# Rotary embedding: GpSimd's two products per tile become one, and the last position is stored as 126 and 2 rows

## The chip, the cores and the metric

The kernel runs on one core of a Trainium2 chip. The metric is the device time of one execution in microseconds, lower is better. Most of it is the span, from the first to the last instruction in the profile.

## The reference

Each row of 64 numbers is cut into two halves of 32 and rotated by an angle that depends on its position alone:

```python
# x: (8, 2048, 8, 64) f32; cos, sin: (2048, 32) f32
x1, x2 = x[..., :32], x[..., 32:]
out1 = x1 * cos - x2 * sin
out2 = x1 * sin + x2 * cos
return np.concatenate([out1, out2], axis=-1)
```

Input and output are 33.55 MB each and every element of x is read once, so the work is two products and one sum per element beside the transfers.

## The kernel before

**Layout.** Each of the 8 batches is one tile of 128 partitions. Partition q holds 16 neighbouring positions (R = 16), a position holds 8 heads of 64 numbers (HD = 512 elements, 2 KB), so a partition's row of a batch is 8192 elements, 32 KB, contiguous in HBM. The unit of computing is UNIT = 4 positions, 2048 elements per partition. The first batch starts with two half units and the last one ends with two half units.

**Tables.** cos_sb, sin_sb and nsin (minus sine) lie in SBUF, 16 x 32 elements per partition. cos_ps and sin_ps are copies in PSUM. ScalarE makes nsin (L90), sin_ps (L91) and neye (L92, minus the identity matrix); VectorE makes cos_ps (L93).

**One tile.** The function rotate computes t1 = x * cos for all elements on VectorE (L129), and t2 = the other half times the signed sine on GpSimd in two products (L122): the second halves of t2 from the first halves of x and sin_sb, then the first halves of t2 from the second halves of x and nsin. Each product writes 32 of every 64 elements and repeats the table over the 8 heads. Then out = t1 + t2, in the place of x. There are three kinds of tile:

- A, the most: VectorE adds (L136).
- B, the first tile of batches 2, 4 and 5: TensorE adds by two products with the identity matrix (L143, L144), ScalarE copies the sum from PSUM (L145).
- C, the first tile of batches 1 and 3: VectorE makes t2 too (L148), TensorE adds (L160, L161), ScalarE copies (L165). GpSimd has no part in it.

**Order of the work.** Every instruction keeps its place in the program's order on its engine. All loads of x are issued by SP (L67), the load of cos after the first of them (L69); sin is loaded by ScalarE's queue (L76). Five batches fit in SBUF (NBUF = 5); the load of batch b + 5 waits until the store of batch b has landed. Stores (L74) are issued by ScalarE's queue, one for a whole batch of 4 MB, except that batch 0 is stored in three parts. The last batch is stored by SP, in parts of 8, 4 and 4 positions, each when the pieces that it covers are done. At the end (L219) SP waits for all stores to have landed.

Of the kernel before, what the change touches and what calls it, by code (L numbers as in the profile page):

```python
# [9 lines left out]
@with_exitstack  # L10
def kernel(
    ctx: ExitStack,
    tc: tile.TileContext,
    x: bass.AP,
    cos: bass.AP,
    sin: bass.AP,
    out: bass.AP,
):
    nc = tc.nc
    keep = tc.keep_in_program_order  # L20
    f32 = mybir.dt.float32
    PSUM = bass.MemoryType.PSUM

    B, S, H, D = x.shape
    Dh = D // 2
    P = 128
    HD = H * D
    R = S // P
    ROW = R * HD
    UNIT = 4 * HD  # L30
    NBUF = 5
    C = 512
    last = B - 1

    xv = x.rearrange("b (q r) h d -> b q (r h d)", q=P)
    ov = out.rearrange("b (q r) h d -> b q (r h d)", q=P)
    cos_src = cos.rearrange("(q r) d -> q r d", q=P)
    sin_src = sin.rearrange("(q r) d -> q r d", q=P)

    const_pool = ctx.enter_context(tc.tile_pool(name="const", bufs=1))  # L40
    tab_pool = ctx.enter_context(tc.tile_pool(name="tab", bufs=1, space=PSUM))
    t1_pool = ctx.enter_context(tc.tile_pool(name="t1p", bufs=1, space=PSUM))
    o_pool = ctx.enter_context(tc.tile_pool(name="op", bufs=1, space=PSUM))
    t1s_pool = ctx.enter_context(tc.tile_pool(name="t1s", bufs=2))
    xpool = ctx.enter_context(tc.tile_pool(name="xpool", bufs=NBUF))
    t2_pool = ctx.enter_context(tc.tile_pool(name="t2p", bufs=3))

    cos_sb = const_pool.tile([P, R, Dh], f32, tag="cb")
    sin_sb = const_pool.tile([P, R, Dh], f32, tag="sb")
    nsin = const_pool.tile([P, R, Dh], f32, tag="ns")  # L50
    eye = const_pool.tile([P, P], f32, tag="eye")
    neye = const_pool.tile([P, P], f32, tag="neye")
    cos_ps = tab_pool.tile([P, R, Dh], f32, tag="cp")
    sin_ps = tab_pool.tile([P, R, Dh], f32, tag="sp")

    xts = {}

    def spans(sizes):
        lo = 0
        for n in sizes:  # L60
            yield lo, n
            lo += n

    def load(b):
        xt = xpool.tile([P, ROW], f32, tag="xt", name=f"xt{b}")
        for lo, n in spans([UNIT, UNIT, 2 * UNIT] if b == 0 else [ROW]):
            keep(nc.sync.dma_start(out=xt[:, lo : lo + n], in_=xv[b, :, lo : lo + n]))  # L67
            if b == 0 and lo == 0:
                keep(nc.sync.dma_start(out=cos_sb, in_=cos_src))  # L69
        xts[b] = xt  # L70

    def store(b, lo, n):
        queue = nc.sync if b == last else nc.scalar
        keep(queue.dma_start(out=ov[b, :, lo : lo + n], in_=xts[b][:, lo : lo + n]))  # L74

    keep(nc.scalar.dma_start(out=sin_sb, in_=sin_src))  # L76
    for b in range(NBUF):
        load(b)

    keep(nc.gpsimd.memset(eye, 0.0))  # L80
    nc.gpsimd.affine_select(
        out=eye,
        in_=eye,
        compare_op=mybir.AluOpType.not_equal,
        fill=1.0,
        base=0,
        pattern=[[-1, P]],
        channel_multiplier=1,
    )
    keep(nc.scalar.mul(nsin, sin_sb, -1.0))  # L90
    keep(nc.scalar.copy(sin_ps, sin_sb))  # L91
    keep(nc.scalar.mul(neye, eye, -1.0))  # L92
    keep(nc.vector.tensor_copy(cos_ps, cos_sb))  # L93

    def rep(a, n):
        return dataclasses.replace(a, ap=[a.ap[0][:], a.ap[1][:], [0, n], a.ap[-1][:]])

    kinds = {}
    for b, kind in ((1, "C"), (2, "B"), (3, "C"), (4, "B"), (5, "B")):
        kinds[(b, 0)] = kind  # L100

    def rotate(b, lo, n):
        kind = kinds.get((b, lo), "A")
        xt = xts[b][:, lo : lo + n]
        r0 = lo // HD
        nr = n // HD
        xk = xt.rearrange("p (r k d) -> p r k d", r=nr, d=Dh)
        xu = xt.rearrange("p (g u d) -> p g u d", u=2, d=Dh)
        if kind == "A":
            t1 = t1_pool.tile([P, n], f32, tag="t1")  # L110
        else:
            t1 = t1s_pool.tile([P, n], f32, tag="t1s")
        if kind == "C":
            t2 = t1s_pool.tile([P, n], f32, tag="t1s")
        else:
            t2 = t2_pool.tile([P, n], f32, tag="t2")
        t1u = t1.rearrange("p (g u d) -> p g u d", u=2, d=Dh)
        t2u = t2.rearrange("p (g u d) -> p g u d", u=2, d=Dh)
        if kind != "C":
            for u, tab in ((1, sin_sb), (0, nsin)):  # L120
                keep(
                    nc.gpsimd.tensor_mul(  # L122
                        out=t2u[:, :, u, :].rearrange("p (r h) d -> p r h d", h=H),
                        in0=xu[:, :, 1 - u, :].rearrange("p (r h) d -> p r h d", h=H),
                        in1=rep(tab[:, r0 : r0 + nr, :], H),
                    )
                )
        keep(
            nc.vector.tensor_mul(  # L129
                out=t1.rearrange("p (r k d) -> p r k d", r=nr, d=Dh),  # L130
                in0=xk,
                in1=rep(cos_ps[:, r0 : r0 + nr, :], 2 * H),
            )
        )
        if kind == "A":
            keep(nc.vector.tensor_add(out=xt, in0=t1, in1=t2))  # L136
        elif kind == "B":
            for j in range(n // (2 * C)):
                o = o_pool.tile([P, 2 * C], f32, tag="o")
                for k in range(2):  # L140
                    cs = slice((2 * j + k) * C, (2 * j + k + 1) * C)
                    oc = o[:, k * C : (k + 1) * C]
                    nc.tensor.matmul(oc, eye, t1[:, cs], start=True, stop=False)  # L143
                    nc.tensor.matmul(oc, eye, t2[:, cs], start=False, stop=True)  # L144
                keep(nc.scalar.copy(xt[:, 2 * j * C : 2 * (j + 1) * C], o))  # L145
        else:
            keep(
                nc.vector.tensor_mul(  # L148
                    out=t2.rearrange("p (r k d) -> p r k d", r=nr, d=Dh),
                    in0=xk,  # L150
                    in1=rep(sin_ps[:, r0 : r0 + nr, :], 2 * H),
                )
            )
            G = C // Dh
            for u in range(2):
                o = o_pool.tile([P, n // 2], f32, tag="o")
                for j in range(n // 2 // C):
                    oc = o[:, j * C : (j + 1) * C]
                    gs = slice(j * G, (j + 1) * G)
                    nc.tensor.matmul(oc, eye, t1u[:, gs, u, :], start=True, stop=False)  # L160
                    nc.tensor.matmul(  # L161
                        oc, eye if u else neye, t2u[:, gs, 1 - u, :], start=False, stop=True
                    )
                keep(
                    nc.scalar.copy(  # L165
                        xu[:, :, u, :], o.rearrange("p (g d) -> p g d", d=Dh)
                    )
                )

    def pieces(b):  # L170
        if b == 0:
            return [2 * HD, 2 * HD, UNIT, UNIT, UNIT]
        if b == last:
            return [UNIT, UNIT, UNIT, 2 * HD, 2 * HD]
        return [UNIT] * 4

    def shares(b):
        if b == 0:
            return [UNIT, UNIT, 2 * UNIT]
        if b == last:  # L180
            return [2 * UNIT, UNIT, UNIT]
        return [ROW]

    for b in range(B):
        done = 0
        outs = list(spans(shares(b)))
        for lo, n in spans(pieces(b)):
            rotate(b, lo, n)
            done = lo + n
            while outs and sum(outs[0]) <= done:  # L190
                store(b, *outs.pop(0))
        if b + NBUF <= last:
            load(b + NBUF)
# [30 lines left out]
```

## Time and profile before

| | |
|---|---|
| time, median of 3 runs | 163.39 us (163.34 to 163.5) |
| time of the profiled execution | 163.35 us |
| its span | 161.5 us |
| instructions in the span | 460 |
| HBM read and written | 34.08 MB and 33.55 MB, 419 GB/s over the span |
| VectorE, product with cos on 2048 elements (L129) | x30, 68.5 us, 2291 ns each |
| VectorE, sum on 2048 elements (L136) | x25, 57.3 us, 2292 ns each |
| GpSimd, product with sin_sb on 1024 elements (L122) | x28, 66.2 us, 2365 ns each, 3.2 us idle before |
| GpSimd, product with nsin on 1024 elements (L122) | x28, 66.3 us, 2368 ns each |
| VectorE's waits for GpSimd before L136 | 1.2 us, 2 times |
| last sum of VectorE begins | 150.98 us, 1.23 us long |
| last parts of the last batch, from issue to landing | 13.5 us for 2 MB; 9.9 us (median of two) for 1 MB |

Times inside the profile count from the start of the span. The time of a run is longer than the span by what lies around it, 163.35 - 161.5 = 1.85 us in the profiled execution. The 16 DMA engines of the core share every transfer: a store of 128 rows shows 16 completions. GpSimd's instructions overlap a little in the records, so what counts for its speed is the distance from one start to the next.

### The profile page before, as it was taken

The numbers are of one execution on the slowest core, as the hardware profiler recorded it, in microseconds if no ns is written. First come the engines' busy times: TensorE is split into PE (matmuls) and PEld (weight loads), VectorE is DVE, ScalarE is ACT, GpSimd is POOL, SyncE is SP. The second block draws the span as 40 slices with busy tenths as digits, with TensorE's granted clock in tenths as the row PEclk, the third lists the DMA queues.
The fourth block names the chain that finished last, engine by engine and source line by source line (L and its number), as shares of the span: only waits on it lengthen the run. The fifth ranks groups of instructions, "written<-read, shape, count | busy, mean of one in ns | idle before, by whom it ended". The sixth has DMA issues, their size and how long they took to land.

```text
span 161.5 us, 460 instructions
## 1 busy us (share of the span) xinstructions
PE 49.2 (30%) x80; PEld 18.5 (11%) x80; DVE 140.1 (87%) x66; ACT 12.8 (8%) x14; POOL 138.9 (86%) x70
## 2 busy tenths in 40 slices
PE   0000000597309770978039723973000000000000
PEld 0000000142004220323023302320000000000000
DVE  0297999999999999999999999999999999999600
ACT  3300000002200220021100220022000000000000
POOL 1399997999999999999994999999999999996000
PEclk9999999999975998589956995599655555555555
DMA  5999998998999999999999999999999999999994
GB/s 153 423 458 418 430 487 381 430 487 381 487 398 446 389 462 389 462 446 389 487 422 389 487 416 389 487 422 398 473 422 406 471 422 406 471 422 406 426 404 209
DMA packets 3458, 67.65 MB, mean 419 GB/s; under 512 B 384, under 2 KB 384, under 8 KB 640
## 3 DMA queue, kind: packets, MB, share of 16 engines
q1 hardware_dynamic: 2016, 38.01, 55.3%
q10 hardware_dynamic: 1440, 29.62, 42.8%
q14 instruction: 2, 0.02, 0.0%
HBM read 34.08 MB, written 33.55 MB: 419 GB/s over the span
## 4 chain that ended last, share of the span: by engine, by line
DVE 75%; POOL 9%; issue 6%; DMA 4%; DVEq 0%
DVE t L129 40%; DVE xt L136 33%; POOL t L122 9%; DMA sin_sb<-in_sin_dram 4%; DVE t L148 3%; DVEq L136 0%
## 5 line engine op out<-in xcount | busy, mean ns | idle before, releaser
L122 POOL TENSOR_TENSOR t<-xt,sin_sb 128x1024 f32<-128x1024 f32 (+1 forms) x32 | 71.2, 2226 | 8.5 <-DMA sin_sb<-in_sin_dram 5.3
L129 DVE TENSOR_TENSOR t<-xt,cos_ps 128x2048 f32<-128x2048 f32 (+1 forms) x34 | 73.4, 2166 | 0.8
L122 POOL TENSOR_TENSOR t<-xt,nsin 128x1024 f32<-128x1024 f32 (+1 forms) x32 | 71.3, 2228 | 0.0
L136 DVE TENSOR_TENSOR xt<-t,t 128x2048 f32<-128x2048 f32 (+1 forms) x29 | 62.2, 2145 | 4.2 <-POOL t L122 1.2
L143 PE MATMUL o<-t,eye 128*128 128x512 f32 x24 | 16.9, 797 | 23.1 <-DVE t L129 19.7
L160 PE MATMUL o<-t,eye 128*128 128x512 f32 x16 | 12.0, 842 | 37.9 <-DVE t L129 35.7
L144 PE MATMUL o<-t,eye 128*128 128x512 f32 x24 | 14.9, 709 | 0.0
L145 ACT COPY xt<-o 128x1024 f32<-128x1024 f32 x6 | 6.1, 1012 | 45.7 <-PE o L144 45.7
L143 PEld LDWEIGHTS o<-t,eye 128*128 128x128 f32 x24 | 5.5, 256 | 32.5 <-issue 26.6
L160 PEld LDWEIGHTS o<-t,eye 128*128 128x128 f32 x16 | 3.7, 256 | 43.4 <-issue 39.5
L165 ACT COPY xt<-o 128x1024 f32<-128x1024 f32 x4 | 4.0, 1012 | 47.8 <-PE o L161 47.8
L93 DVE COPY cos_ps<-cos_sb 128x512 f32<-128x512 f32 x1 | 0.7, 695 | 7.1 <-DMA cos_sb<-in_cos_dram 7.1
L144 PEld LDWEIGHTS o<-t,eye 128*128 128x128 f32 x24 | 5.6, 235 | 8.1 <-issue 8.1
L161 PE MATMUL o<-t,neye 128*128 128x512 f32 x8 | 6.2, 872 | 0.2
L148 DVE TENSOR_TENSOR t<-xt,sin_ps 128x2048 f32<-128x2048 f32 x2 | 4.6, 2280 | 0.0
L161 PE MATMUL o<-t,eye 128*128 128x512 f32 x8 | 4.1, 592 | 0.0
L161 PEld LDWEIGHTS o<-t,neye 128*128 128x128 f32 x8 | 2.1, 296 | 5.2 <-issue 3.6
L161 PEld LDWEIGHTS o<-t,eye 128*128 128x128 f32 x8 | 1.5, 190 | 1.9 <-issue 1.9
L90 ACT ACT_TABLE_LOAD x1 | 1.3, 1283 | 1.2 <-PEq L208 1.2
L90 ACT ACTIVATE nsin<-sin_sb 128x512 f32<-128x512 f32 x1 | 0.6, 630 | 4.1 <-DMA sin_sb<-in_sin_dram 4.1
L91 ACT COPY sin_ps<-sin_sb 128x512 f32<-128x512 f32 x1 | 0.6, 578 | 0.0
L80 POOL MEMSET eye<- 128x128 f32 x1 | 0.2, 204 | 0.3 <-POOLq L208 0.3
(6 smaller groups left out, 1.0 us busy)
## 6 DMA issues: line engine op xcount, KB each, us to landing
xt<-in_x_dram SPq DMA_DIRECT2D x7, 4096.0 KB, 34.5
out_dram<-xt ACTq DMA_DIRECT2D x6, 4096.0 KB, 30.5
xt<-in_x_dram SPq DMA_DIRECT2D x2, 1024.0 KB, 6.8
xt<-in_x_dram SPq DMA_DIRECT2D x1, 2048.0 KB, 12.3
out_dram<-xt ACTq DMA_DIRECT2D x2, 1024.0 KB, 19.3
out_dram<-xt ACTq DMA_DIRECT2D x1, 2048.0 KB, 28.0
out_dram<-xt SPq DMA_DIRECT2D x1, 2048.0 KB, 13.5
out_dram<-xt SPq DMA_DIRECT2D x2, 1024.0 KB, 9.9
```

Of the source, the lines that this page charges most:

```text
L90: keep(nc.scalar.mul(nsin, sin_sb, -1.0))
L93: keep(nc.vector.tensor_copy(cos_ps, cos_sb))
L122: nc.gpsimd.tensor_mul(out=t2u[:, :, u, :].rearrange("p (r h) d -> p r h d", h=H), in0=xu[:, :, 1 - u, :].rearrange("p (r h) d -> p r h d" ...
L129: nc.vector.tensor_mul(out=t1.rearrange("p (r k d) -> p r k d", r=nr, d=Dh), in0=xk, in1=rep(cos_ps[:, r0 : r0 + nr, :], 2 * H),)
L136: keep(nc.vector.tensor_add(out=xt, in0=t1, in1=t2))
L143: nc.tensor.matmul(oc, eye, t1[:, cs], start=True, stop=False)
L144: nc.tensor.matmul(oc, eye, t2[:, cs], start=False, stop=True)
L145: keep(nc.scalar.copy(xt[:, 2 * j * C : 2 * (j + 1) * C], o))
L148: nc.vector.tensor_mul(out=t2.rearrange("p (r k d) -> p r k d", r=nr, d=Dh), in0=xk, in1=rep(sin_ps[:, r0 : r0 + nr, :], 2 * H),)
L160: nc.tensor.matmul(oc, eye, t1u[:, gs, u, :], start=True, stop=False)
L161: nc.tensor.matmul(oc, eye if u else neye, t2u[:, gs, 1 - u, :], start=False, stop=True)
L165: nc.scalar.copy(xu[:, :, u, :], o.rearrange("p (g d) -> p g d", d=Dh))
```

## The change

**One product on GpSimd.** A new table sgn of 16 x 2 x 32 elements holds minus sine and sine side by side, made by ScalarE with a product and a copy. Except for the very first tile, which keeps its two products, GpSimd makes t2 with one product of the tile's full size: the output is contiguous, x is read with its two halves exchanged (from the second half, a step of -32 elements to the first), and sgn is repeated over the heads. nsin is gone, and cos_sb and sin_sb lie in the two buffers of the pool t1s, which kinds B and C use later.

**The last store.** The last part of the last batch, 4 positions, becomes a part of 3 positions and a part of 1. The function store sends a part of one position as two DMAs, of partitions 0 to 125 and of partitions 126 and 127.

```diff
-    cos_sb = const_pool.tile([P, R, Dh], f32, tag="cb")
-    sin_sb = const_pool.tile([P, R, Dh], f32, tag="sb")
-    nsin = const_pool.tile([P, R, Dh], f32, tag="ns")
+    cos_sb = t1s_pool.tile([P, R, Dh], f32, tag="t1s", name="cos_sb")
+    sin_sb = t1s_pool.tile([P, R, Dh], f32, tag="t1s", name="sin_sb")
+
+    sgn = const_pool.tile([P, R, 2, Dh], f32, tag="sg")
...
         queue = nc.sync if b == last else nc.scalar
-        keep(queue.dma_start(out=ov[b, :, lo : lo + n], in_=xts[b][:, lo : lo + n]))
+
+        parts = (slice(0, 126), slice(126, P)) if n == HD else (slice(0, P),)
+        for p in parts:
+            keep(queue.dma_start(out=ov[b, p, lo : lo + n], in_=xts[b][p, lo : lo + n]))
...
-    keep(nc.scalar.mul(nsin, sin_sb, -1.0))
+    keep(nc.scalar.mul(sgn[:, :, 0, :], sin_sb, -1.0))
+    keep(nc.scalar.copy(sgn[:, :, 1, :], sin_sb))
...
     def rep(a, n):
-        return dataclasses.replace(a, ap=[a.ap[0][:], a.ap[1][:], [0, n], a.ap[-1][:]])
+        return dataclasses.replace(a, ap=[a.ap[0][:], a.ap[1][:], [0, n]] + [d[:] for d in a.ap[2:]])
...
-        if kind != "C":
-            for u, tab in ((1, sin_sb), (0, nsin)):
+        if (b, lo) == (0, 0):
+            for u, tab in ((1, sin_sb), (0, sgn[:, :, 0, :])):
...
+        elif kind != "C":
+            x5 = xt.rearrange("p (r h u d) -> p r h u d", r=nr, h=H, u=2)
+            dims = [d[:] for d in x5.ap[:3]] + [[-Dh, 2], x5.ap[4][:]]
+            keep(
+                nc.gpsimd.tensor_mul(
+                    out=t2.rearrange("p (r h u d) -> p r h u d", r=nr, h=H, u=2),
+                    in0=dataclasses.replace(x5, offset=x5.offset + Dh, ap=dims),
+                    in1=rep(sgn[:, r0 : r0 + nr], H),
+                )
+            )
...
-            return [2 * UNIT, UNIT, UNIT]
+            return [2 * UNIT, UNIT, 3 * HD, HD]
```

## The prediction

> **What bounds the kernel now.** I first read the engines' totals: two engines are busy for seven eighths of the span, which would make this a VectorE or GpSimd kernel.
>
> ```profile
> PE 49.2 (30%) x80; PEld 18.5 (11%) x80; DVE 140.1 (87%) x66; ACT 12.8 (8%) x14; POOL 138.9 (86%) x70
> ```
>
> The DMA queues correct that. The two data queues hold 55.3% + 42.8% = 98.1% of what 16 DMA engines can do in the whole span. The last line, two packets of instructions, comes back below.
>
> ```profile
> q1 hardware_dynamic: 2016, 38.01, 55.3%
> q10 hardware_dynamic: 1440, 29.62, 42.8%
> q14 instruction: 2, 0.02, 0.0%
> ```
>
> Next the windows (start:end, length, busy time of PE, PEld, DVE, ACT, POOL, clock, then the DMA engines' share and GB/s): is any DMA time free?
>
> ```profile
> 4.00:157.00 153.00, 49.24 (x80) 18.53 (x80) 140.11 (x66) 11.47 (x13) 138.22 (x64) 0.77 1.00 431
> 157.00:159.50 2.50, 0.00 (x0) 0.00 (x0) 0.00 (x0) 0.00 (x0) 0.00 (x0) 0.50 0.96 406
> ...
> 160.50:161.50 1.00, 0.00 (x0) 0.00 (x0) 0.00 (x0) 0.00 (x0) 0.00 (x0) 0.50 0.00 0
> ```
>
> From 4 to 157 us the share is 1.00 at 431 GB/s: no engine of the sixteen pauses, so in that stretch a faster compute engine can win nothing. The same view in steps of 0.1 us shows how they stop:
>
> ```profile
> 159.40:159.50 0.10, 0.00 (x0) 0.00 (x0) 0.00 (x0) 0.00 (x0) 0.00 (x0) 0.50 0.61 246
> 159.50:159.60 0.10, 0.00 (x0) 0.00 (x0) 0.00 (x0) 0.00 (x0) 0.00 (x0) 0.50 0.03 0
> ...
> 159.70:159.80 0.10, 0.00 (x0) 0.00 (x0) 0.00 (x0) 0.00 (x0) 0.00 (x0) 0.50 0.39 164
> ...
> 160.00:160.10 0.10, 0.00 (x0) 0.00 (x0) 0.00 (x0) 0.00 (x0) 0.00 (x0) 0.50 0.20 82
> ```
>
> A packet is booked where it begins. In the trace's packet records one 8 KB row takes 309 ns and the next begins after 306. So 246 GB/s over 0.1 us are three rows begun before 159.5, ended by 159.74 at the latest; 164 are two rows, on two engines, begun 159.7 to 159.8; 82 is one more row. Fourteen engines are done at 159.74; of **two late ones** one ends near 160.02, the other near 160.36. Its completion releases SP at 160.73, and the exit takes until 161.5.
>
> Why two are late: the completions of each store, 16 per store, lie within 0.48 us of each other up to 90 us (0.35 in the last before that); from the first instruction packet (94.1 us) on one of them is 1.06 us behind, from the second (115.8 us) on another 0.75 us. So each instruction page costs some 0.7 us on the DMA engine that carries it, and nothing catches up, since all are full.
>
> Last, the slack of the compute. The last product is stored at
>
> ```profile
> 152.23 0.33 SPq L74 DMA_DIRECT2D out_dram<-xt  x1
> ```
>
> and the first engine is free of the store before it at 156.96 (its first completion, 157.30, less the 0.34 us that every completion follows its packet). With about 1 us from issue to first packet (the first load: 0.74 to 1.75) that leaves 3.7 us.
>
> **The change part by part.**
>
> GpSimd's product. Starts of successive products:
>
> ```profile
> 138.56 2.32 POOL L122 TENSOR_TENSOR t<-xt,sin_sb 128x1024 f32<-128x1024 f32 x1
> 140.84 2.33 POOL L122 TENSOR_TENSOR t<-xt,nsin 128x1024 f32<-128x1024 f32 x1
> 143.13 1.25 POOL L122 TENSOR_TENSOR t<-xt,sin_sb 128x512 f32<-128x512 f32 x1
> 144.34 1.24 POOL L122 TENSOR_TENSOR t<-xt,nsin 128x512 f32<-128x512 f32 x1
> ```
>
> The pitch is 2.28 for 1024 elements and 1.21 for 512: 1.07 per 512, 0.14 fixed. One product of 2048 is then 4.42 against 2 x 2.28 = 4.56, or 0.14 less on 28 tiles, about 4 us of GpSimd. No row shows a backward step between halves. Bounds: 4.42 below; above, twice the slowest long product (2.456 in the trace), 4.91. I take 4.42, because runs of 32 elements are there already and only their order differs. DVE needs 2.29 + 2.29 + 0.14 of waits = 4.72 per such tile, so the compute stays DVE's and ends perhaps 1 us earlier (DVE's waits for GpSimd total 1.2). Worth **0**: the full DMA engines hide it. Were GpSimd slower, it would use up its own idle time of 3.2 us and then the slack of 3.7, 6.9 / 28 = 0.25 per tile over 4.56: the end moves from 4.81 on.
>
> Start. ACT makes the second half of the table with one more copy (L91's kind, 0.58), so sin_ps and neye, queued behind it, come 0.58 later: sin_ps at about 8.3, needed by DVE at 30.1, neye at 32. GpSimd needs the full table at its third product, 9.09; it is there near 7.7. The first product still reads sin_sb alone. The tables share buffers with t1s, whose first tile is written at 27.9, long after the readers are done. Loads, their order and their queues are unchanged. Worth 0.
>
> Instructions. GpSimd issues 31 products fewer. If one of the two instruction pages is GpSimd's, it goes away or moves to the end: at 94.1 us GpSimd had 59 of its 94 recorded instructions behind it, at 115.8 us 70; afterwards it has about 63 in all. VectorE passes through too (64 and 80 of 113), so which engine fetched can't be read. In the sum: 0.
>
> The last store. Three DMAs replace one. The 3-position part isn't earlier: the piece before ends at position 14, the part at 15. So all three are issued after the last add, some 0.45 apart on SP (0.33 + 0.1), the last about 0.9 later than now; the slack of 3.7 covers it, and nothing is queued on SP behind them but the final waits. Rows, their recorded 309, 611 and 1213 ns less the 3 by which they overlap: 8 KB 306, 16 KB 608, 32 KB 1210, a 2 KB table row 84 - 3 = 81: on that line 6 KB is 231. 126 does not divide by 16, and it does by 14: fourteen engines with 9 rows each, and two with none, if shares are equal. The last store then takes a left-out engine 8 x 231 = 1.85 instead of 8 x 306 = 2.45, **-0.60**; the others 1.85 + 9 x 81 = 2.58, **+0.13**; the two that take the extra rows +0.21. If the left-out ones are the late ones: 160.36 - 0.60 = 159.76, 160.02 - 0.60 = 159.42; of the rest the last is 159.74 + 0.13 = 159.87, or 159.95 if it has an extra row. That ends it, 0.41 to 0.49 earlier than 160.36. If the shares aren't taken so, bounds: from +0.21 up (nobody relieved) to 2.26 / 0.73 below.
>
> The sum: -0.45 on the profiled execution (163.35, span 161.5, 1.85 around it), which stands 0.04 under the median of 163.39. **Forecast 162.95**, -0.27%. A measurement of this kernel can tell about 0.2%, 0.33 us, from no change.
>
> Two rules weigh on it. The Trainium skill, "DMA: Bandwidth & Descriptors", section "Why a DMA increments its semaphore by 16 and not by 1", has a copy take the largest number of engines up to 16 that divides the slowest dimension, lowest-numbered first: 14 engines for 126 rows, 2 for 2. The 16 completions of each 128-row store agree; no run here shows 126 rows. The same page, "Rules for kernel authors", speaks against the change: splitting a transfer by partitions isn't worth it, one 128-partition transfer is better; by it the sum would be 0 or a little over. The skill's "Runtime: NRT & Kernel Launch", section "Instruction fetch mechanics", calls the cost of a page mostly hidden; here the completions show 0.7 us on one DMA engine, unhidden.
>
> **The rivals.**
>
> B. Only the later engine is relieved, by the split or because its page was GpSimd's. The other ends at 160.02 + 0.13 = 160.15: -0.21, **163.18**. For it: GpSimd's shorter program, and that nothing names the late engines. Against: two late, two left out, and 0.60 fits 0.62. The skill's DMA page, "Latency and other measured facts", calls engines 7 and 15 usually the slower; of these the split leaves out only one. Which engines are late here, no row shows.
>
> C. Neither is relieved (other engines, or rows spread over sixteen): 160.36 + 0.13 = 160.49, **163.52**.
>
> D. The other side: the narrow 2 KB rows of the 126-row store collide, because its rows lie on the engines otherwise than a 128-row store's. The table rows, the only ones of 2 KB, took 84 ns mostly, but 225 to 528 while all queues started. At 250 ns nine rows are 2.25: 159.74 - 2.45 + 1.85 + 2.25 = 161.39, +1.03, **164.4**. It decides from (2.45 + 0.62 - 1.85) / 9 = 136 ns per row on, where the slowest of fourteen passes 160.36. Against: the engines are past their start by then.
>
> E. The backward pattern is dear: at 4.91 per tile, (4.91 - 4.81) x 28 = 2.8, **166.2**. For: not in the trace. Against: the same run length.
>
> **How the numbers follow.** Forecast 0.50, B 0.16, C 0.16, D 0.10, E 0.08. The range should leave out D, E and little more: from 162.7 (both late engines relieved and 0.2 less spread among the others than now) to 163.6 (C and the spread of 0.1 of the runs). The forecast alone: 162.85 to 163.1. Faster by over 0.2% means under 163.06: nearly all of the forecast (0.46) and a third of B (0.05), 0.51. Within: the rest of both and C, 0.31. Slower, above 163.72: D and E, 0.18.
>
> **What would show it.** Right: no DMA share after about 159.9, share 1.00 from 4 to 157 as now, GpSimd's product near 4.4 with fewer than 40 of them, the 2 KB rows near 84 ns. The forecast fails if packets still begin after 160.0 (B, C), if the 2 KB rows pass 136 ns (D), or if DVE waits for GpSimd at the end and the last store issues after 156 (E).

## The result and the profile after

The changed kernel takes 163.62 us (median of 22 runs, 163.52 to 163.90), the kernel before 163.39 in the same comparison (22 runs, 163.25 to 163.51). The ratio is 1.0016, with a 95% interval of 1.0009 to 1.0022: slower by 0.23 us, where 162.95, 0.44 faster, was forecast. That is less than the 0.2% which the prediction took as the smallest difference to be told from none, but the interval excludes no difference.

The profiled execution of the changed kernel took 163.66 us with a span of 161.74; before it was 163.35 with 161.55. So 0.19 us of the loss lies inside the span, and **0.12 around it** (1.92 instead of 1.80; the 1.85 given for the kernel before comes from a span rounded to 161.5). Over all runs the time around the span is 1.90 against 1.80, so that of the 0.23 some 0.13 lies inside.

Engines and DMA queues of the changed kernel, from its page:

```profile
PE 49.5 (31%) x80; PEld 18.5 (11%) x80; DVE 140.1 (87%) x66; ACT 13.3 (8%) x15; POOL 136.0 (84%) x39
...
q1 hardware_dynamic: 2160, 38.01, 55.2%
q10 hardware_dynamic: 1440, 29.62, 42.8%
q14 instruction: 1, 0.01, 0.0%
```

GpSimd is down to 39 instructions and 136.0 us, and only one instruction packet (the fetch of a page of an engine's instructions) is left in the span; it begins at 94.13 us. The one that began at 115.84 in the kernel before is gone. GpSimd's products in the order of time, merged by the view (start, length of the stretch):

```profile
97.44 22.45 POOL L137 TENSOR_TENSOR t<-xt,sgn 128x2048 f32<-128x2048 f32 x5 [0.20 <-DVE xt L151]
```

Five of them in 22.45 us, the last 4.53 long: a distance of (22.45 - 4.53) / 4 = 4.48 from start to start, against 4.42 predicted and 4.56 for the two halves before. The windows (start:end, length, busy time of PE, PEld, DVE, ACT, POOL, clock, DMA share, GB/s) show that the DMA engines are as full as before, and what the end looks like:

```profile
4.00:157.00 153.00, 49.46 (x80) 18.50 (x80) 140.11 (x66) 11.99 (x14) 135.31 (x33) 0.77 1.00 431
157.00:159.50 2.50, 0.00 (x0) 0.00 (x0) 0.00 (x0) 0.00 (x0) 0.00 (x0) 0.50 0.97 397
159.50:160.50 1.00, 0.00 (x0) 0.00 (x0) 0.00 (x0) 0.00 (x0) 0.00 (x0) 0.50 0.20 76
```

The steps of 0.1 us at the very end:

```profile
159.80:159.90 0.10, 0.00 (x0) 0.00 (x0) 0.00 (x0) 0.00 (x0) 0.00 (x0) 0.50 0.22 82
159.90:160.00 0.10, 0.00 (x0) 0.00 (x0) 0.00 (x0) 0.00 (x0) 0.00 (x0) 0.50 0.06 21
160.00:160.10 0.10, 0.00 (x0) 0.00 (x0) 0.00 (x0) 0.00 (x0) 0.00 (x0) 0.50 0.05 20
160.10:160.20 0.10, 0.00 (x0) 0.00 (x0) 0.00 (x0) 0.00 (x0) 0.00 (x0) 0.50 0.05 20
160.20:160.30 0.10, 0.00 (x0) 0.00 (x0) 0.00 (x0) 0.00 (x0) 0.00 (x0) 0.50 0.10 41
160.30:160.40 0.10, 0.00 (x0) 0.00 (x0) 0.00 (x0) 0.00 (x0) 0.00 (x0) 0.50 0.05 20
160.40:160.50 0.10, 0.00 (x0) 0.00 (x0) 0.00 (x0) 0.00 (x0) 0.00 (x0) 0.50 0.05 20
160.50:160.60 0.10, 0.00 (x0) 0.00 (x0) 0.00 (x0) 0.00 (x0) 0.00 (x0) 0.50 0.01 0
```

A share of 0.05 to 0.06 is one engine of sixteen. From 159.9 on one engine alone still begins rows: 20 GB/s over 0.1 us are 2 KB, one row at a time (41 where two rows begin in one step). These are rows of the 126-row store. In the packet records this engine ends its last 6 KB row at 159.80, then writes nine 2 KB rows, 80 ns apart, the last begun at 160.445. Its completion follows at 160.86, where the last one before was at 160.71. The late engine, which the split was predicted to leave out, has nine rows more to write.

The 126-row store does spread as the prediction had it: 14 engines complete it, and 2 complete the 2-row store (at 160.19 and 160.22); so not every transfer is shared by all sixteen. Two engines were left out of the 126 rows, but not the late one. The counts, 14 for 126 rows and 2 for 2, agree with the Trainium skill, "DMA: Bandwidth & Descriptors", section "Why a DMA increments its semaphore by 16 and not by 1", which takes the largest number of engines up to 16 that divides the rows.

### The profile page after: what moved, and what is told of

Same layout as the page of the kernel before. It is cut to its first block, busy times and chain, and to the rows that moved or that the text cites. A ratio compares the mean times of both kernels' runs of the same rounds, so it can differ in the third digit from the quotient of the medians.

```text
span 161.7 us, 433 instructions
## 1 busy us (share of the span) xinstructions
PE 49.5 (31%) x80; PEld 18.5 (11%) x80; DVE 140.1 (87%) x66; ACT 13.3 (8%) x15; POOL 136.0 (84%) x39
## 4 chain that ended last, share of the span: by engine, by line
DVE 74%; POOL 9%; issue 7%; DMA 3%; DVEq 0%; POOLq 0%
DVE t L144 40%; DVE xt L151 32%; POOL t L137 7%; DMA xt<-in_x_dram 3%; DVE t L163 3%; POOL t L127 2%; DVEq L151 0%; POOLq L127 0%
## 5 line engine op out<-in xcount | busy, mean ns | idle before, releaser
L137 POOL TENSOR_TENSOR t<-xt,sgn 128x2048 f32<-128x2048 f32 (+1 forms) x31 | 132.9, 4318 | 5.7 <-DVE xt L151 3.7
L158 PE MATMUL o<-t,eye 128*128 128x512 f32 x24 | 18.3, 856 | 24.6 <-DVE t L144 21.2
L175 PE MATMUL o<-t,eye 128*128 128x512 f32 x16 | 10.4, 735 | 36.8 <-DVE t L144 34.6
L159 PE MATMUL o<-t,eye 128*128 128x512 f32 x24 | 15.8, 746 | 0.0
L158 PEld LDWEIGHTS o<-t,eye 128*128 128x128 f32 x24 | 5.6, 256 | 34.5 <-issue 28.1
L175 PEld LDWEIGHTS o<-t,eye 128*128 128x128 f32 x16 | 3.4, 235 | 42.0 <-issue 38.2
L159 PEld LDWEIGHTS o<-t,eye 128*128 128x128 f32 x24 | 6.3, 263 | 9.1 <-issue 9.1
L127 POOL TENSOR_TENSOR t<-xt,sin_sb 128x512 f32<-128x512 f32 x1 | 1.3, 1267 | 5.2 <-DMA xt<-in_x_dram 5.2
L176 PE MATMUL o<-t,eye 128*128 128x512 f32 x8 | 4.1, 592 | 0.0
L176 PEld LDWEIGHTS o<-t,eye 128*128 128x128 f32 x8 | 1.5, 190 | 1.9 <-issue 1.9
L127 POOL TENSOR_TENSOR t<-xt,sgn 128x512 f32<-128x512 f32 x1 | 1.3, 1266 | 0.0
L94 ACT ACTIVATE sgn<-sin_sb 128x512 f32<-128x512 f32 x1 | 0.6, 630 | 3.7 <-DMA sin_sb<-in_sin_dram 3.7
L95 ACT COPY sgn<-sin_sb 128x512 f32<-128x512 f32 x1 | 0.6, 602 | 0.0
```

Of the source, the lines that this page charges most:

```text
L94: keep(nc.scalar.mul(sgn[:, :, 0, :], sin_sb, -1.0))
L127: nc.gpsimd.tensor_mul(out=t2u[:, :, u, :].rearrange("p (r h) d -> p r h d", h=H), in0=xu[:, :, 1 - u, :].rearrange("p (r h) d -> p r h d" ...
L137: nc.gpsimd.tensor_mul(out=t2.rearrange("p (r h u d) -> p r h u d", r=nr, h=H, u=2), in0=dataclasses.replace(x5, offset=x5.offset + Dh, ap ...
L176: nc.tensor.matmul(oc, eye if u else neye, t2u[:, gs, 1 - u, :], start=False, stop=True)
```

## The experiments

The theory made from these traces, T: one late DMA engine sets the end; the fetch of a page of VectorE's instructions (VectorE's page, for short) makes it late; it isn't one of the two left out, so it gets 9 rows more. Rivals: R1, the product and its tables cost the time; R2, more DMAs at the end cost by their issue and completion, whatever share of the rows each engine gets.

**One product alone** (e1). The changed kernel with the last store of before:

```diff
-        parts = (slice(0, 126), slice(126, P)) if n == HD else (slice(0, P),)
+        parts = (slice(0, P),)
...
-            return [2 * UNIT, UNIT, 3 * HD, HD]
+            return [2 * UNIT, UNIT, UNIT]
```

> The changed kernel with the last store of before (one part of 4 positions). Theory T (one late DMA engine sets the end; it carries VectorE's instruction page of 94 us, is not one of the two left out, and gets 9 rows of 2 KB more): GpSimd's page of 116 us is gone and with it the second late engine, but the first one ends at 160.36 as before, so 163.39, within 0.1. Rival R1 (the product, its table or the shared buffers cost the time): 163.6 here too.

Measured: 163.52, ratio 1.0009 (1.0000 to 1.0017), between what T and R1 expected. The span is the one of before, 161.52 in the profiled execution; the time around it is 1.93. The steps at the end show one late engine instead of two:

```profile
159.70:159.80 0.10, 0.00 (x0) 0.00 (x0) 0.00 (x0) 0.00 (x0) 0.00 (x0) 0.50 0.20 82
...
160.00:160.10 0.10, 0.00 (x0) 0.00 (x0) 0.00 (x0) 0.00 (x0) 0.00 (x0) 0.50 0.19 82
```

82 GB/s over 0.1 us are one 8 KB row, begun at 159.7 and again at 160.0; before there were two in the first of these steps. So in the span the product costs nothing, as T says, and the second late engine is gone. What it costs lies outside the span; the interval of e1 by itself begins at no difference.

**The store alone** (e2). The kernel before with the changed store:

```diff
-        keep(queue.dma_start(out=ov[b, :, lo : lo + n], in_=xts[b][:, lo : lo + n]))
+        parts = (slice(0, 126), slice(126, P)) if n == HD else (slice(0, P),)
+        for p in parts:
+            keep(queue.dma_start(out=ov[b, p, lo : lo + n], in_=xts[b][p, lo : lo + n]))
...
-            return [2 * UNIT, UNIT, UNIT]
+            return [2 * UNIT, UNIT, 3 * HD, HD]
```

> The kernel before with the changed last store (3 positions, then 126 and 2 rows) alone. T: two instruction packets as before, two late engines, both later by 0.13 to 0.17, the end 160.5; with SP's last waits 163.6. R1: 163.39 or less.

Measured: 163.54, ratio 1.0014 (1.0006 to 1.0023), with two instruction packets (94.04 and 115.83 us), a span of 161.65 and 1.81 around it. The steps:

```profile
160.00:160.10 0.10, 0.00 (x0) 0.00 (x0) 0.00 (x0) 0.00 (x0) 0.00 (x0) 0.50 0.10 41
160.10:160.20 0.10, 0.00 (x0) 0.00 (x0) 0.00 (x0) 0.00 (x0) 0.00 (x0) 0.50 0.11 41
160.20:160.30 0.10, 0.00 (x0) 0.00 (x0) 0.00 (x0) 0.00 (x0) 0.00 (x0) 0.50 0.05 20
160.30:160.40 0.10, 0.00 (x0) 0.00 (x0) 0.00 (x0) 0.00 (x0) 0.00 (x0) 0.50 0.05 20
160.40:160.50 0.10, 0.00 (x0) 0.00 (x0) 0.00 (x0) 0.00 (x0) 0.00 (x0) 0.50 0.01 0
```

In the first step two engines begin a row each; in the second one engine begins two, 80 ns apart, and goes on until 160.43. In the packet records both late engines write nine 2 KB rows, the last begun at 160.05 and 160.35: neither was left out. R1 as the only cause falls here.

**Three positions and one, all rows** (e3). The kernel before with the list [2 * UNIT, UNIT, 3 * HD, HD] and nothing else.

> The kernel before; the last part stored as 3 positions and 1, both with all 128 rows. T: every engine has 8 rows of 6 KB and 8 of 2 KB, 8 x 0.231 + 8 x 0.080 = 2.49 for 2.45, so +0.04, and up to +0.06 in SP's last waits: 163.4 to 163.5. Rival R2 (more DMAs at the end cost by their issue and completion, whatever their shares): 163.55 or more.

Measured: 163.48, ratio 1.0011 (1.0001 to 1.0022). The median fits T better than R2, but the intervals of e2 and e3 overlap, so times alone don't separate a ninth row from the cost of more DMAs. The traces do. From the last completion of the store before to the last of all it takes 2.42 us in the kernel before, 2.40 in e1, 2.45 in e3, and 2.53 in e2 and in the changed kernel: cutting the part into 3 and 1 positions costs 0.03, where T had 0.04, and a ninth row 0.08 more, the 80 ns of one row. What is left of R2 is SP's end: its last wait begins 0.06 us after the last completion in e2, in e3 and in the changed kernel, and 0.02 after it before. (In e3's profiled execution two completions of one store were already 1.4 us behind at 70 us; from 130 us on its lags are like those of the kernel before, so its end can be compared.)

**Which engines are late: staircases** (e4, e5). The kernel before; the last position of batch 5, stored in mid-run while both late engines lag, is cut into DMAs of few rows. If a DMA of n rows runs on the first n engines, it has a straggler (a completion that comes late) as long as a late engine's number, counted from 0, is below n.

```diff
+        parts = [slice(0, P)]
+        if n == HD:
+            parts, at = [], 0
+            for rows in (*range(16, 4, -1), 2):
+                parts.append(slice(at, at + rows))
+                at += rows
...
+        if b == 5:
+            return [15 * HD, HD]
```

> The kernel before; the last position of batch 5 is stored by 13 DMAs of 16, 15, 14 ... 5 and 2 rows, which tells the late engines' numbers if n rows go to the first n engines: the completions of a DMA with n rows have a straggler of 0.6 to 1.1 us as long as n is over the number of a late engine, and none below it. T: two numbers, the one of the 94 us page between 2 and 13 (it got 9 rows in the changed kernel and no tenth), and none of them both 14 and 15. If the prediction's placing had been right: stragglers only with 16 and 15 rows. Time 163.4 to 164.

Measured: 166.49. With 16 rows and every number down to 10, three completions come about 0.5, 0.7 to 0.8 and 1.03 to 1.06 us after the first, the others within 0.4. None of these engines has a number from 10 up. The DMAs of 9 rows and fewer were issued only after the queues had run dry, and tell nothing; this is also where the 3 us went:

```profile
136.00:140.00 4.00, 0.00 (x0) 0.00 (x0) 3.97 (x2) 0.00 (x0) 4.00 (x3) 0.50 0.92 391
140.00:144.00 4.00, 0.00 (x0) 0.00 (x0) 3.86 (x3) 0.00 (x0) 4.00 (x3) 0.50 0.36 135
```

A share of 0.36 means engines without work: ScalarE's queue was still issuing the small DMAs (until 143.2), and the store of batch 6 stood behind them. So e5 goes on from 9 rows, with (80, 9, 8, 7, 6, 5, 4, 9) in place of the range:

> The kernel before; the last position of batch 5 is stored by DMAs of 80, 9, 8, 7, 6, 5, 4 and 9 rows. With 16 to 10 rows both stragglers were among the completions, so both late engines have numbers below 10. Here the straggler of the 94 us page goes out of the completions of a DMA with n rows at its number n, and so does that of the 116 us page; T: neither was left out by 126 rows, so both numbers lie in 0 to 9, the first one not 0 or 1. If rows aren't dealt to the first n engines, stragglers come and go without an order. Time 164 to 167, as the last of these DMAs wait.

Measured: 165.43. From the trace's completion records, the time after the first data completion of each DMA, in us:

```text
rows  the rest within   stragglers
 9         0.20         0.65  0.76  0.98
 8         0.21         0.63  0.76  0.97
 7         0.23         0.62  0.77  0.98
 6         0.09         0.63  0.78  0.98
 5         0.05         0.62  0.79  0.99
 4         0.05         0.62        0.99
```

There is an order, as if each smaller DMA ran on part of the larger one's engines: the straggler of 0.78 goes out between 5 and 4 rows, so it is on engine 4. The latest, 0.98, which has lagged since VectorE's page (at 96.5 us in this execution), is still there with 4 rows; it is one of 0 to 3. It isn't 0 or 1 either: the 2-row store completed at 160.06 and 160.11 in e2, which has the same pages, while the late engine completed at 160.77 (160.22 and 160.86 in the changed kernel). The late engine is **number 2 or 3** in this order. Which of the other two carries the second page can't be told apart here, and one of them lagged before that page came; both have numbers of 4 or below, and a 126-row store gives rows to all of them.

**Whose page: fewer matmuls, and padding** (e6, e7). In e6, on top of e1, VectorE adds the first tile of batch 5, so TensorE has 16 pairs of products and weights less.

```diff
-    for b, kind in ((1, "C"), (2, "B"), (3, "C"), (4, "B"), (5, "B")):
+    for b, kind in ((1, "C"), (2, "B"), (3, "C"), (4, "B")):
```

> The one product with the store of before (as e1), and the first tile of batch 5 added by VectorE instead of TensorE: 8 of 40 pairs of TensorE's products less after 94 us, and 2.4 us more of VectorE, inside the slack of 3.7. If the page of 94 us is TensorE's (135 of its 172 recorded instructions lie before it) and is fetched when it gets near, it goes away, no engine is late, the end is 159.7 and the time 162.8 to 163.0. If it is VectorE's: as e1, 163.5, or 163.6 with the later last store. If VectorE's 2.4 us aren't hidden: 164 or more.

Measured: 163.46, ratio 1.0000 (0.9989 to 1.0011), and the page is still fetched, at 96.40 (as late in e3, e5 and e10, which leave VectorE's and TensorE's work alone). So it isn't TensorE's, if a page is fetched when its engine gets near it. The 2.4 us more of VectorE are hidden. In e7, on top of e1, VectorE gets 12 one-element fills at the start:

```diff
+    pad = const_pool.tile([P, 1], f32, tag="pad")
+    for _ in range(12):
+        keep(nc.vector.memset(pad, 0.0))
     keep(nc.vector.tensor_copy(cos_ps, cos_sb))
```

> As e1, with 12 one-element fills on VectorE in its idle time before 7 us. If the page of 94 us is VectorE's, its fetch comes 12 recorded instructions earlier, which is 16 to 20 us, near 75; if it is another engine's it stays at 94. Time as e1 in both cases, 163.4 to 163.6.

Measured: 163.66, 0.06 over what was expected (a single run). The queues of e7 between 73.0 and 74.5 us hold the packet:

```profile
q1 hardware_dynamic: 16, 0.52, 83.1%
q14 instruction: 1, 0.01, 1.3%
```

It begins at 73.55, 20.5 us earlier than in e1 (94.07), for 12 instructions more ahead of it. The page is **VectorE's**. And from 75.0 us on, 34 us earlier than in e1, one completion of each transfer is 1.0 us late: the lag follows the page. The lag is 1.06 us at 75 us and 1.06 in the last store: once gained it stays, and the end comes no earlier (last completion at 160.90, in e1 at 160.69).

**GpSimd's page** (e8). On top of e1, 31 fills on GpSimd while it waits for the first data:

```diff
+    for _ in range(31):
+        keep(nc.gpsimd.memset(pad, 0.0))
```

> As e1, with 31 one-element fills on GpSimd in its idle time before 6 us, so that it has as many instructions as before the change, and all of them earlier. If the page of 116 us was GpSimd's, a second instruction packet is back, at a time when GpSimd passes its 70th recorded instruction, and with it a second late engine; the time around the span, 1.92 us in the two kernels with one product and 1.81 in the three with two, falls back to 1.81, and the time to 163.4. If the product itself costs the 0.1: 163.5 and 1.92 as in e1.

Measured: 163.40, ratio 0.9999 (0.9982 to 1.0016). A second instruction packet is back, here in the queues between 74 and 76 us:

```profile
q1 hardware_dynamic: 16, 0.52, 61.3%
q14 instruction: 1, 0.01, 1.0%
```

It begins at 74.88, when GpSimd has passed 67 recorded instructions (70 at the second page of the kernel before), and from 89.7 us on one completion of each transfer lags by 0.70 us; VectorE's page (94.30) then adds one of 1.06.

The two pages don't cost the same. The 32 KB row that begins right behind VectorE's packet took 1744 to 1751 ns in all thirteen traces, the row behind GpSimd's 1427 to 1435 ns in the seven that have it, and most such rows take 1213. With the packet's 306 ns that makes 0.84 and 0.53 us of delay on the DMA engine that carries it. Why the row behind the packet is longer, no run shows.

The time around the span is down to 1.82. Over all runs of each kernel (mean of a run's time less its span):

```text
instruction packets in the span   kernel            around the span, us
two                               before            1.80
two                               e2 store alone    1.81
two                               e3 3 and 1        1.80
two                               e8 padded         1.81
two                               e11 (below)       1.81
one                               e1 product alone  1.93
one                               e6                1.91
one                               changed kernel    1.90
two                               e4, e5 (1 run)    1.99, 2.13
one                               e7 (1 run)        1.96
one                               e9, e10           2.06, 2.02
```

Among the kernels that differ in GpSimd's instructions alone (e1 and e8, the changed kernel and e11) the 0.1 appears when GpSimd's page isn't fetched within the span, and goes when it is. It isn't the only thing that counts: e4 and e5, with many more DMAs on ScalarE's queue, and e9 and e10, with a DMA on GpSimd's, have more around the span than either group. That the page is then fetched after the span is not shown: e4 and e9 have an instruction packet 1.8 to 1.9 us after their spans' end, but e4 has both pages in the span as well, and in e1 no such packet is recorded.

**The change and the padding** (e11). The changed kernel with the 31 fills.

> The changed kernel with the 31 fills of e8 on GpSimd. If the change's loss has two parts that add up, 9 rows more on the late engine (+0.15 to 0.2 in the span) and GpSimd's page fetched after the span (+0.12 around it), the second goes and the first stays: time around the span 1.80, two instruction packets in the span, 163.5. If the time around the span has another cause in the changed kernel: 1.92 and 163.6.

Measured: 163.53 (163.47 to 163.89), 1.81 around the span, two packets in it. That is what was expected of the kernel. The runs of before beside it were scattered (median 163.59, 163.25 to 164.35), so the ratio, 0.9992 (0.9977 to 1.0007), says nothing.

**Relieving the right engine** (e9, e10). As e1, the last position as 126 and 2 rows, the 126 issued by GpSimd; in e9 a load of 4 short rows, which nothing uses, is issued by GpSimd first.

```diff
+            q = nc.gpsimd if p.stop == 126 else queue
+            keep(q.dma_start(out=ov[b, p, lo : lo + n], in_=xts[b][p, lo : lo + n]))
...
+    turn = const_pool.tile([4, Dh], f32, tag="turn")
+    keep(nc.gpsimd.dma_start(out=turn, in_=cos[0:4, :]))
```

> As e1 (one product), the last position stored as 126 and 2 rows as in the change, but the 126 rows are issued by GpSimd, and a load of 4 short rows that nothing uses is issued by GpSimd at the start. The staircases put the late engine of VectorE's page at 2 or 3. If GpSimd's transfers are dealt on in turn (4 rows to the first four engines, 126 rows to the fourteen after these), 2 and 3 are the two left out: the late engine ends at 160.36 - 0.60 = 159.76, the others at 159.9, and the time is 163.52 - 0.4 = 163.1, under both kernels. If they start from the first engine again, or are spread over all sixteen: as the changed kernel, 163.6. If GpSimd's issuing costs at the end: 164 or more.

> As e9 without the load of 4 rows. If transfers are dealt on in turn from the first engine, the 126 rows leave out 14 and 15, the late engine gets 9 rows more as in the changed kernel: 163.6, 0.4 to 0.5 over e9. If the order has nothing to do with it: the same as e9.

Measured: 163.86, ratio 1.0028 (1.0012 to 1.0044), and 163.84, ratio 1.0031 (1.0013 to 1.0049). A miss: the two are the same, and neither is relieved. GpSimd's DMA moves the 126 rows in 63 packets of 4 KB, two rows each, and shows 16 completions; nine rows on each of 14 engines would leave an odd row on every one, and no single row of it is recorded. So it doesn't use 14 engines with equal shares. Of the 0.2 us over the changed kernel more than half lies around the span (2.06 and 2.02 on average, against 1.90). No run leaves out engine 2 or 3 alone: in the order of the staircase a DMA on fewer engines keeps the low numbers. So **it stays open** whether relieving the late engine brings the 0.4 us of the prediction. No version here is measurably faster than the kernel before.

## Why the prediction was wrong

**What bounds it: right.** The DMA engines are full from 4 to 157 us in every kernel but the staircases, the end is set by one engine that an instruction page made late (e7 moved the page, and the lag with it), and 2.4 us more of VectorE cost nothing (e6).

**GpSimd's product: right to 0.06 us.** 4.48 from start to start instead of 4.42, worth nothing inside the span (e1). Rival E's dear pattern didn't come.

**The start: right.** e1's span is that of before.

**The last store: the step that failed** is "if the left-out ones are the late ones". The sizes were near: fourteen engines with 9 rows, two with none, 80 ns a row. Rival D didn't come either: the 2 KB rows took 84 ns. But the late engine is number 2 or 3 in the order of the staircase, and the fourteen engines of the 126 rows include it. So the -0.60 went to engines that had time, and the +0.13 to the one that sets the end: its last packet ended at 160.53 instead of 160.36, +0.17, its completion 0.15 later, where rival C had +0.13. The fit of "two late, two left out, 0.60 for 0.62" was a coincidence of sizes, and half of the chance was put on it. Another 0.04 us came from SP: its last wait began 0.02 us after the last completion before, 0.06 after it now, as another wait still follows the one that ends last.

**The instructions: half right.** One page was GpSimd's, as the prediction thought possible, and it left the span; but it was the earlier-ending of the two late engines, so rival B didn't follow, and the sum's 0 for the span holds. The size was near as well: "some 0.7" a page, where the packets have 0.84 and 0.53. **The term that was missing** is the time around the span, taken as fixed (at 1.85, 1.80 unrounded): it grew by 0.12, 0.10 over all runs. This is somewhat less than half of the loss, and e8 and e11 tie it to GpSimd's page or to the number of its instructions, which change together.

**The sum, made again:** +0.19 in the span from the store and +0.12 around it from the product, 0.31 on the profiled executions; over all runs the medians differ by 0.23, and e1 and e2 alone by 0.15 and 0.17, with intervals of 0 to 0.28 and 0.10 to 0.38. Rival C, with the right mechanism at 163.52, lacked the 0.12.

**The rules of the Trainium skill.** "Two transfers to disjoint partition halves" aren't worth it (the Trainium skill, "DMA: Bandwidth & Descriptors", section "Rules for kernel authors") agrees, with +0.17 for e2, though e3, which cuts by positions alone, has +0.11 of it. The same page's engines 7 and 15 as usually the slower ones (section "Latency and other measured facts") don't appear here: the three latest have numbers of 4 and below, and two of them are late by an instruction page. That page of the Trainium skill ties these two engines, as a best guess, to the transfers that GpSimd issues, and this kernel has none.

## What to carry to other kernels

Here every DMA engine was full, and the end belonged to the engine that carried something extra. Before moving bytes away from such an engine, find out its number, by DMAs of few rows whose completions show the straggler: two engines left out can be the wrong two. Cutting instructions on an engine can take an instruction page out of the span and still leave the time around the span longer (1.90 for 1.80 here), so compare that too. And a coincidence of two sizes is no evidence for a place.

## What the runs showed of the hardware

- An instruction packet of 8 KB takes 309 ns, and the 32 KB row right behind it takes 1745 ns (VectorE's page) or 1434 (GpSimd's) for 1213. The DMA engine that carries it stays behind the others for the rest of a saturated run (the latest completion of a store went from 0.37 to 1.07 us after the first in the kernel before; to 1.06 from 75 us on when the page came at 73.6 us).
- VectorE's page came on DMA engine 2 or 3, counted in the order in which a staircase of smaller DMAs keeps them; the three latest engines there have numbers of 4 and below.
- SP took 0.33 us to issue the 128-row store of 6 KB rows, 0.82 for 126 rows of 2 KB right behind it (1.22 in e11) and 0.56 for the 2 rows behind those (e3: 1.06 for 128 rows of 2 KB).
- A GpSimd-issued store of 126 rows of 2 KB went out in packets of 4 KB and showed 16 completions, where SP's showed 14.
